# Attention steps of a decoder trunk: one broadcast VectorE product for the probabilities, and value products evacuated by ScalarE and added by GpSimd

## The chip, the cores and the metric

One Trainium2 chip, one core. The time is the device time of one launch in microseconds; the kernel before is given as the median of three runs. The engines are TensorE (PE in the profile, its weight loads PEld), VectorE (DVE), ScalarE (ACT), GpSimd (POOL) and the DMA queue of SyncE (SP). Each works through its own instruction list in order and waits on semaphores for the others.

## The reference

A two-layer causal decoder trunk over 512 tokens of 1024 features in float32. Layer 0 mixes tokens with a gated MLP in chunks of 128, then a gated MLP with a causal convolution of width 3, then a gated per-layer embedding. A shared key and value projection follows. Layer 1 has sliding-window attention over these, then the same two blocks again, then a final norm. The change lies in the attention:

```python
q = (xn @ w_q).reshape(B, nb, BLOCK, N_KV_HEADS, GQA_GROUP, HEAD_DIM)
scores = einsum('bnikgd,bnjkd->bnkgij', q, kblk) * HEAD_DIM ** -0.5
scores = scores - slopes * dist            # ALiBi
scores = where(valid, scores, -inf)        # 128 keys back, inside two blocks of 128
m = maximum(max(scores), sink)
e = exp(scores - m)
probs = e / (sum(e) + exp(sink - m))
out = einsum('bnkgij,bnjkd->bnikgd', probs, vblk)
return out.reshape(B, S, N_Q_HEADS * HEAD_DIM) @ w_o
```

There are 16 query heads of 64 features in 4 groups (4 heads share a key and value head), and 4 blocks of 128 tokens.

## The kernel before

The activations lie feature by token. Every large product is made of three matmuls on operands split in a rounded high part and the rest (`h*w` as `hi*hi + lo*hi + hi*lo`, L181 to L183), so each operand needs a cast on ScalarE (L154 for weights, L252 for activations) and a subtraction on VectorE (L155, L253).

The attention is a list of 16 steps, step i = 4g + n for head group g and token block n. The loop at L864 issues for each i: `scores(i)`, the work put beside step i (`fill`), `mix(i-2)`, `turn(i-1)` and `weights(i)`, so three steps are in flight. A scheduler then sets the order on each engine: it runs the program through with costs of its own, and `scores`, `turn` and `weights` have priority.

- `scores(i)`: eight matmuls (L781, L782) into two PSUM tiles `sc`; VectorE chooses between the two key blocks (`copy_predicated`, L784) and takes bias and row extreme (L788, four); ScalarE takes the exponential and its sum (L793, four). A small GpSimd copy (L774) puts the sink beside the row. The result lies in `prs`, in one of two buffers.
- `weights(i)`: the reciprocal of the sums `ds` (L801) and four products of 128x128, one per head: the first on VectorE (L807), three on ScalarE (L805).
- `turn(i)`: four TensorE transposes into a PSUM tile `tr` (L822), evacuated as high and low part (`pts`, L252 and L253). For n > 0, two GpSimd masks (L830) make a second pair for the previous block.
- `mix(i)`: two or four value matmuls (L844) into `pv`. Their left operand holds the values' high part in its first 64 columns and the low part in the last 64, so the upper and lower 64 partitions of `pv` have to be added. ScalarE copies the lower half to `side` (L848), VectorE adds the upper half to it, 64x256 twice (L852), placing the heads in the two partition halves. The sum is split: `oh` by ScalarE (L856), `ol` by GpSimd, for the last step by VectorE (L857). Both are columns of the tiles `o2`, two of them per head group.
- Beside the steps, TensorE has the query projections of the later groups (`project`, in step 0 to 9) and the merges, the w_o products on `o2` (`merge`, tile `o`, from step 10 and after the last step). A merge reads a whole `o2` tile, and so needs all four steps of its group.

PSUM has eight tiles, which all these share in turn.

Of the kernel before, what the change touches and what calls it, by code (L numbers as in the profile page):

```python
# [10 lines left out]
AF = mybir.ActivationFunctionType  # L11
ALU = mybir.AluOpType

P = 128
D = 1024
S = 512
# [10 lines left out]
GQ = HEADS // GROUPS  # L27
# [21 lines left out]
def tile_yoco(ctx: ExitStack, tc: tile.TileContext, t, out: bass.AP, out_b: bass.AP):  # L49
    nc = tc.nc  # L50
# [10 lines left out]
    def psum(name):  # L61
        return mmp.tile([P, S], F32, tag="mm", name=name)
# [166 lines left out]
    ps = psum("idle").rearrange("p (a b) -> p a b", a=4)  # L229
# [331 lines left out]
    for c in range(4):  # L561
# [4 lines left out]
        for j in range(2):  # L566
            m = 2 * c + j
            ps = ups[j]
# [24 lines left out]
    ps = psum("turned")  # L593
# [18 lines left out]
    sides = [slice(0, HD), slice(HD, P)]  # L612
# [184 lines left out]
    def weights(i):  # L797

        pr, sm = live[i]
        ds = at.tile([P, GQ], F32, tag="ds", bufs=2, name=f"ds{i}")  # L800
        nc.vector.reciprocal(ds, sm)  # L801
        for e in range(GQ):
            a, r = pr[:, e, :P], ds[:, e : e + 1]
            if e:
                nc.scalar.activation(a, a, AF.Copy, scale=r)  # L805
            else:
                nc.vector.tensor_scalar_mul(a, a, r)  # L807
        live[i] = pr

    def pair(name):  # L810
# [24 lines left out]
    def mix(i):  # L835
        g, n = steps[i]
        pts = live.pop(i)
        ps = psum(f"pv{i}")
        todo = []
        for b, halves in enumerate(pts):  # L840
            both_halves = (diffs[g][:, n - 1] if b else vt[:, n, g]).rearrange("p a d -> p (a d)")
            todo += [(both_halves, x) for x in halves]
        for j, (lhs, rhs) in enumerate(todo):
            nc.tensor.matmul(ps, lhs, rhs, start=j == 0, stop=j == len(todo) - 1)  # L844


        low = side[sides[0], i % 2 * S : (i % 2 + 1) * S]
        nc.scalar.copy(low, ps[sides[1], :])  # L848
        o = side[:, 2 * S + i % 2 * N : 2 * S + (i % 2 + 1) * N].rearrange("p (b t) -> p b t", b=2)
        a, low = (x.rearrange("p (b e t) -> p e b t", b=2, e=2) for x in (ps[sides[0], :], low))  # L850
        for e in range(2):
            nc.vector.tensor_add(o[sides[e]], a[:, e], low[:, e])  # L852
        cols = slice(n * P, (n + 1) * P)
        for b in range(2):
            oh, ol = o2[2 * g + b]
            nc.scalar.copy(oh[:, cols], o[:, b, :])  # L856
            (nc.vector if i == last - 1 else nc.gpsimd).tensor_sub(ol[:, cols], o[:, b, :], oh[:, cols].bitcast(F32))  # L857

    last = len(steps)
    side = at.tile([P, 4 * S], F32, tag="vtl", name="side")  # L860
# [3 lines left out]
    for i in range(last + 2):  # L864
        if i < last:
            with tc.high_priority():
                scores(i)
        if i <= last:
            fill(i)
        if i >= 2:  # L870
            mix(i - 2)
        if i > last:
            fill(i)
        if 0 <= i - 1 < last:
            with tc.high_priority():
                turn(i - 1)
        if i < last:
            with tc.high_priority():
                weights(i)
# [46 lines left out]
    for i in range(2):  # L926
# [4 lines left out]
        for q in range(2):  # L931
            ps = psum(f"ht{i}_{q}")
# [4 lines left out]
    for m in range(4):  # L937
        ps = psum(f"gate{4 + m}")[:, :N]
# [32 lines left out]
    def gate_t(i, n):  # L971

        c0, w = cuts[i][n]
        ps = psum(f"gt{i}_{n}")[:, :w]
        end = i == 1 and n == len(cuts[i]) - 1
        if end:
            nc.tensor.matmul(ps, rows[:, :P], rows[:, P : 3 * P], start=True, stop=False)
        mm3t(ps, xs, parts2 if c0 >= S else parts, c0 % S, w, 2 + i, first=not end)
        return ps
# [57 lines left out]
    ps = gate_t(0, 1)  # L1037
# [72 lines left out]
```

## Time and profile before

| | |
|---|---|
| median of three runs | 1141.24 us (1140.78 to 1141.5) |
| the profiled execution | 1141.22 us, span 1139.5 us |
| granted TensorE clock | 0.998 |
| TensorE busy | 1127.0 us, 99% of the span |
| VectorE, ScalarE, GpSimd busy | 749.6, 530.0, 107.7 us |
| attention steps | about 592 to 690 us of the span |

Times below are microseconds from the start of the span unless marked ns. A row of the timeline gives start, duration, engine, line, operation, output <- inputs, shapes and a count where like rows are merged; in brackets the idle time before it and what ended it. A busy TensorE is one with an instruction in flight: a matmul's record is longer than the distance to the next one's start. A row of groups gives busy time, mean duration in ns, and idle time before with what ended it. Where a group has "least/median/most", these are ns.

### The profile page before, as it was taken

Reading aid. Unit: us, or ns where it says so; the run is one execution under the profiler, and the core shown is the slowest. Engines: PE = TensorE matmul, PEld = TensorE weight load, DVE = VectorE, ACT = ScalarE, POOL = GpSimd, SP = SyncE. Lnnn points to the kernel's source line nnn. Section 1 sums busy time; section 2 is a strip of 40 time slices with the busy share of each in tenths; the row PEclk is TensorE's granted clock in tenths of the full one; section 3 lists DMA queues with packets and bytes.
Section 4 is the critical chain, followed back from the end, with each engine's and each line's share of the span. In section 5 each row is a group of like instructions: output and inputs, shape, how many; then the busy total and the mean of one; then the engine's idle time right before and its main releaser. Section 6 shows DMA issues by size and latency. Waiting matters only on the chain.

```text
span 1139.5 us, 13604 instructions
## 1 busy us (share of the span) xinstructions
PE 1127.0 (99%) x5266; PEld 940.5 (83%) x5266; DVE 749.6 (66%) x1158; ACT 530.0 (47%) x875; POOL 107.7 (9%) x175
## 2 busy tenths in 40 slices
PE   9999999999999999999999999999999999999997
PEld 7888888888888888888898878888888888888896
DVE  7366477763677367557988977777636763675675
ACT  6533344441344234445657985444313432355562
POOL 2000200000000000021213343000000000000222
PEclk9999999999999999999999999999999999999999
DMA  8422323223223322432224315223223233224302
GB/s 298 145 83 74 111 75 111 101 85 111 78 98 102 111 76 86 134 107 79 74 75 129 93 38 185 98 88 111 78 107 110 66 102 111 93 80 160 111 1 75
DMA packets 25776, 115.41 MB, mean 101 GB/s; under 512 B 2920, under 2 KB 8176, under 8 KB 16240
## 3 DMA queue, kind: packets, MB, share of 16 engines
q1 hardware_dynamic: 25152, 113.89, 29.8%
q8 instruction: 41, 0.67, 0.2%
q10 hardware_dynamic: 560, 0.66, 0.2%
q14 instruction: 23, 0.19, 0.1%
HBM read 108.24 MB, written 2.11 MB: 97 GB/s over the span
## 4 chain that ended last, share of the span: by engine, by line
PE 95%; DVE 2%; issue 1%; ACT 1%; DMA 1%; POOL 0%; SPq 0%; POOLq 0%; DVEq 0%; ACTq 0%
PE up L181 14%; PE up L183 14%; PE up L182 14%; PE d L183 8%; PE d L181 8%; PE d L182 8%; PE gate L181 2%; PE gate L183 2%; PE gate L182 2%; PE u L182 1%; PE u L183 1%; PE u L181 1%; PE o L182 1%; PE o L181 1%; PE o L183 1%; PE q L181 1%
## 5 line engine op out<-in xcount | busy, mean ns | idle before, releaser
L154 ACT CAST wh<-wraw 128x1024 fp32r<-128x1024 f32 (+2 forms) x197 | 202.0, 1028 | 264.6 <-PE d L182 131.0
L155 DVE TENSOR_TENSOR wl<-wraw,wh 128x1024 fp32r<-128x1024 f32 (+1 forms) x198 | 238.4, 1205 | 127.9 <-ACT wh L154 127.6
L181 PE MATMUL up<-nf00h,wh 128*128 128x512 f32 x352 | 137.1, 390 | 0.0
L181 PE MATMUL up<-nf10h,wh 128*128 128x512 f32 x352 | 137.0, 389 | 0.0
L182 PE MATMUL up<-nf00l,wh 128*128 128x512 f32 x352 | 136.9, 389 | 0.0
L183 PE MATMUL up<-nf00h,wl 128*128 128x512 f32 x352 | 136.9, 389 | 0.0
L183 PE MATMUL up<-nf10h,wl 128*128 128x512 f32 x352 | 136.9, 389 | 0.0
L182 PE MATMUL up<-nf10l,wh 128*128 128x512 f32 x352 | 136.9, 389 | 0.0
L181 PE MATMUL d<-ah,wh 128*128 128x512 f32 x352 | 136.9, 389 | 0.0
L182 PE MATMUL d<-al,wh 128*128 128x512 f32 x352 | 136.9, 389 | 0.0
L183 PE MATMUL d<-ah,wl 128*128 128x512 f32 x352 | 136.9, 389 | 0.0
L379 ACT ACTIVATE c<-hs,vec 128x512 f32<-128x512 f32 x88 | 71.5, 815 | 72.0 <-DVE hs L375 71.2
L380 DVE SCALAR_TENSOR_TENSOR c<-hs,vec,c 128x511 f32<-128x511 f32 x88 | 65.8, 749 | 34.5 <-ACT c L379 34.4
L355 DVE TENSOR_TENSOR h<-h,d 128x512 f32<-128x512 f32 x56 | 38.4, 686 | 73.8 <-PE d L183 73.8
L252 ACT CAST ah<-a 128x512 fp32r<-128x512 f32 x44 | 27.4, 622 | 109.5 <-DVE a L385 109.4
L183 PEld LDWEIGHTS up<-nf10h,wl 128*128 128x128 f32 x352 | 66.1, 188 | 13.8
L182 PEld LDWEIGHTS d<-al,wh 128*128 128x128 f32 x352 | 66.1, 188 | 13.8
L183 PEld LDWEIGHTS up<-nf00h,wl 128*128 128x128 f32 x352 | 66.1, 188 | 13.8
L183 PEld LDWEIGHTS d<-ah,wl 128*128 128x128 f32 x352 | 66.1, 188 | 13.7
L182 PEld LDWEIGHTS up<-nf00l,wh 128*128 128x128 f32 x352 | 66.1, 188 | 13.7
L182 PEld LDWEIGHTS up<-nf10l,wh 128*128 128x128 f32 x352 | 66.1, 188 | 13.7
L181 PEld LDWEIGHTS d<-ah,wh 128*128 128x128 f32 x352 | 66.1, 188 | 13.6
(454 smaller groups left out, 2061.7 us busy)
## 6 DMA issues: line engine op xcount, KB each, us to landing
wraw<-in_w_up SPq DMA_DIRECT2D x44, 1024.0 KB, 4.8
wraw<-in_w_down SPq DMA_DIRECT2D x16, 896.0 KB, 4.6
wraw<-in_w_down SPq DMA_DIRECT2D x8, 1024.0 KB, 4.8
wraw<-in_w_gate SPq DMA_DIRECT2D x8, 1024.0 KB, 4.8
wraw<-in_w_u SPq DMA_DIRECT2D x4, 1024.0 KB, 5.9
wraw<-in_w_out SPq DMA_DIRECT2D x4, 1024.0 KB, 4.8
wraw<-in_w_q SPq DMA_DIRECT2D x4, 1024.0 KB, 4.9
wraw<-in_w_o SPq DMA_DIRECT2D x4, 1024.0 KB, 4.9
```

What stands on the lines that cost most here:

```text
L154: nc.scalar.copy(hi, src)
L155: nc.vector.tensor_sub(low, src, hi.bitcast(F32))
L181: nc.tensor.matmul(ps, wh[:, a:b], xh, start=st, stop=False)
L182: nc.tensor.matmul(ps, wh[:, a:b], xl, start=False, stop=False)
L183: nc.tensor.matmul(ps, wl[:, a:b], xh, start=False, stop=en)
L252: nc.scalar.copy(hi, src)
L355: nc.vector.tensor_add(h[m], h[m], ps)
L379: nc.scalar.activation(c, hs, AF.Identity, bias=v("conv_b", l * 2 * NJ + col), scale=cw[2])
L380: nc.vector.scalar_tensor_tensor(c[:, 1:], hs[:, : S - 1], cw[1], c[:, 1:], op0=ALU.mult, op1=ALU.add)
```

## The change

Two places of the attention steps change, and nothing else.

In `weights` the four products become one: VectorE multiplies the whole 128 x 4 x 128 block of `prs` with `ds`, repeated along the last axis. ScalarE has no part in it any more.

In `mix` ScalarE copies both halves of `pv` to `side`, both into the same 64 partitions, the lower or the upper half in turn with the step. The two sums of 64x256, now with both inputs in SBUF, go to GpSimd. `oh` and `ol` stay where they were.

```diff
         nc.vector.reciprocal(ds, sm)
-        for e in range(GQ):
-            a, r = pr[:, e, :P], ds[:, e : e + 1]
-            if e:
-                nc.scalar.activation(a, a, AF.Copy, scale=r)
-            else:
-                nc.vector.tensor_scalar_mul(a, a, r)
+        a = pr[:, :, :P]
+        nc.vector.tensor_mul(a, a, ds.rearrange("p (e o) -> p e o", o=1).to_broadcast([P, GQ, P]))
...
-        low = side[sides[0], i % 2 * S : (i % 2 + 1) * S]
-        nc.scalar.copy(low, ps[sides[1], :])
         o = side[:, 2 * S + i % 2 * N : 2 * S + (i % 2 + 1) * N].rearrange("p (b t) -> p b t", b=2)
-        a, low = (x.rearrange("p (b e t) -> p e b t", b=2, e=2) for x in (ps[sides[0], :], low))
+        two = [side[sides[i % 2], x * S : (x + 1) * S] for x in range(2)]
+        for x in range(2):
+            nc.scalar.copy(two[x], ps[sides[x], :])
+        a, low = (x.rearrange("p (b e t) -> p e b t", b=2, e=2) for x in two)
         for e in range(2):
-            nc.vector.tensor_add(o[sides[e]], a[:, e], low[:, e])
+            nc.gpsimd.tensor_add(o[sides[e]], a[:, e], low[:, e])
```

In the changed kernel the product is L803, the copies L846, the sums L849, the transposes L818, the masks L826, the value matmuls L840, `oh` L853 and `ol` L854. The scheduler orders the instructions anew.

## The prediction

> **What bounds the kernel now.** I read the page's head first, then the busy time of each engine in stretches, then TensorE's waits, then the timeline of the stretch where they lie.
>
> ```profile
> PE 1127.0 (99%) x5266; PEld 940.5 (83%) x5266; DVE 749.6 (66%) x1158; ACT 530.0 (47%) x875; POOL 107.7 (9%) x175
> ```
>
> TensorE is the bound over the whole: 1127.0 us of a span of 1139.5. Whatever the change does to other engines counts only where TensorE waits for them. In stretches (columns: stretch, length, busy us of PE, PEld, DVE, ACT, POOL, granted clock, DMA):
>
> ```profile
> 640.00:650.00 10.00, 9.89 (x55) 8.17 (x54) 8.83 (x32) 9.30 (x29) 4.84 (x10) 1.00 0.24 52
> 650.00:660.00 10.00, 8.37 (x49) 6.62 (x50) 9.51 (x40) 9.79 (x37) 3.27 (x8) 1.00 0.25 54
> 660.00:670.00 10.00, 8.78 (x45) 6.76 (x44) 7.80 (x26) 8.85 (x31) 5.45 (x12) 1.00 0.30 106
> 670.00:680.00 10.00, 9.31 (x45) 7.33 (x46) 8.01 (x29) 7.92 (x30) 5.16 (x8) 1.00 0.01 2
> 600.00:690.00 90.00, 86.33 (x453) 70.80 (x452) 72.75 (x235) 72.77 (x236) 35.73 (x74) 1.00 0.35 104
> ```
>
> The attention steps (600 to 690 us) hold 90 - 86.33 = 3.67 us of idle TensorE, nearly all between 640 and 680, where ScalarE and VectorE are busy up to 98% and 95%. GpSimd is idle for more than half. The clock is full, so it plays no part. What TensorE waits for, from its list of waits and its timeline:
>
> ```profile
> PE tr L822 <- DVE prs L807: 1.7, 3, 0.8
> 639.83 0.39 PE L183 MATMUL q<-n11h,wl 128*128 128x512 f32 x1
> 640.06 0.39 PE L181 MATMUL q<-n11h,wh 128*128 128x512 f32 x1
> 649.50 0.39 PE L844 MATMUL pv<-pts,vt 128*128 128x512 f32 x1
> 650.68 0.41 PE L822 MATMUL tr<-ident,prs 128*128 128x128 f32 x2 [0.80 <-DVE prs L807]
> 662.11 0.50 PE L182 MATMUL o<-ol,wh 128*128 128x512 f32 x1 [0.71 <-POOL ol L857]
> 670.03 0.52 PE L822 MATMUL tr<-ident,prs 128*128 128x128 f32 x3 [0.53 <-DVE pts L253]
> 672.20 0.47 PE L844 MATMUL pv<-p13h,vt 128*128 128x512 f32 x1 [0.36 <-ACT prs L793]
> 672.92 0.50 PE L181 MATMUL o<-oh,wh 128*128 128x512 f32 x1 [0.26 <-ACT oh L856]
> ```
>
> Unstalled matmuls start 0.23 us apart (639.83, 640.06) though each record lasts 0.39, so each stall is 0.16 us longer than its idle mark: from 649.50 to 650.68 TensorE lost 1.18 - 0.23 = 0.95 us, not 0.80. There are three stalls of the transposes on the scaled probabilities (1.7 + 3 x 0.16 = 2.2 us), one where a merge (w_o product) waits for the last `ol` of step 7 (0.9), and three after step 11 (0.53 + 0.36 + 0.26 + 3 x 0.16 = 1.6). With the small ones the attention loses 3.67 + some 8 x 0.16 = 5.0 us. That is 0.44% of the time and all that this change can win.
>
> **The change part by part.** Groups from 590 to 692 us (last two figures before the idle time: busy us in all, mean ns of one), and the nearest rows for the new operations (ns: least, median, most):
>
> ```profile
> L793 ACT ACTIVATE prs<-prs,neg 128x129 f32<-128x129 f32 x64 | 25.2, 396 | 3.2 <-DVE neg L788 2.4 <-POOL ol L857 0.6
> L805 ACT ACTIVATE prs<-prs,ds 128x128 f32<-128x128 f32 x48 | 15.9, 395 | 0.0
> L807 DVE TENSOR_SCALAR prs<-prs,ds 128x128 f32<-128x128 f32 x16 | 6.5, 409 | 0.2
> L848 ACT COPY side<-pv 64x512 f32<-64x512 f32 x16 | 9.3, 583 | 2.9 <-PE pv L844 2.4
> L852 DVE TENSOR_TENSOR side<-pv,side 64x256 f32<-64x256 f32 x32 | 13.3, 416 | 3.8 <-ACT side L848 3.4
> L857 POOL TENSOR_TENSOR ol<-side,oh 128x128 fp32r<-128x128 f32 x30 | 14.1, 490 | 4.3 <-ACT oh L856 4.2
> L335 DVE TENSOR_TENSOR nf0dh<-ident,nf0rh x1: 684/684/684, 153.2 to 153.2; 128x512 fp32r<-128x512 f32 x1
> L912 POOL TENSOR_TENSOR facc<-facc,fsq x6: 737/741/1021, 1104.7 to 1113.4; 128x256 f32<-128x256 f32 x6
> 649.21 0.49 ACT L856 CAST oh<-side 128x128 fp32r<-128x128 f32 x2
> 649.58 0.87 POOL L857 TENSOR_TENSOR ol<-side,oh 128x128 fp32r<-128x128 f32 x2
> 652.12 0.40 PE L844 MATMUL pv<-pts,vt 128*128 128x512 f32 x1
> 653.90 0.58 ACT L848 COPY side<-pv 64x512 f32<-64x512 f32 x1
> 654.39 0.99 ACT L805 ACTIVATE prs<-prs,ds 128x128 f32<-128x128 f32 x3
> ```
>
> VectorE: 16 products of 128x128 (6.5 us) and 32 sums (13.3 us) go; 16 products of 128x512 with a broadcast factor come, priced by L335, which has that shape and that broadcast: 16 x 0.684 = 10.9. Net -8.9 us of 72.75.
>
> ScalarE: the three scalings of a step take 0.99 us end to end; the added copy takes 0.49, since the next instruction starts that long after it (653.90 to 654.39). Net -0.5 us a step, -8 us of 72.77 over 16 steps.
>
> GpSimd: 32 sums of 64x256 come. No row has 64 partitions, or an output in other partitions than the input; the nearest is L912, the same 256 elements on 128 partitions: 0.74 us, 32 x 0.74 = 23.7 us, so 35.73 becomes 59 of 90. Bounds: the 0.49 of a 128x128 `ol`, and L912's 1.02. I take 0.74, the row of equal length.
>
> So the two full engines are relieved by 0.5 us a step and the idle one is filled. Two chains per step change. *Scores to transposes*: reciprocal, then one VectorE product of 0.68 in place of 0.99 on ScalarE: the last transpose can go 0.3 us sooner, the first 0.3 later. *Value product to merge*: copy 0.58, sums 0.83, `oh` 0.49, `ol` 0.87 becomes copies 1.07, sums 1.48, `oh` 0.49, `ol` 0.87: 2.8 us becomes 3.9. A late sum also holds what stands behind `oh` in ScalarE's queue, the next exponentials and evacuations: between copies and `oh` stand mostly two exponentials (0.8), so ScalarE waits some 0.7 us for the sums where it is not late by other work. That can eat its whole 0.5 us a step. VectorE loses such a wait: the sums stood in its queue ahead of scores.
>
> TensorE's instruction order is the same up to the transposes of step 9; then merges move ahead. Merge matmuls between the transposes of steps 9, 10, 11, 12, 13, 14, 15: before 6, 3, 21, 0, 3, 33; after 12, 9, 9, 0, 18, 18.
>
> *Up to the transposes of step 11*: six more merges at steps 10 and 11 are 1.4 us each, against stalls of 0.5 to 0.95; at step 9 ScalarE's new order has all four exponentials ahead of step 8's evacuation, where the last stood behind. So the three stalls on the products go: -2.2 us. The merge on step 7's `ol` now comes six merges (1.4), one value matmul (0.2) and a block of transposes and scores (650.68 to 652.12, 1.4) after that step's value product, 3.0 us, against 3.5 to the first half of `ol`: 0.5 in place of 0.9. Together -2.6.
>
> *After step 11*: the first merge that needs its `oh` comes 8 scores, 4 transposes and two value matmuls after that step's last value product.
>
> ```profile
> 668.63 0.63 PE L844 MATMUL pv<-pts,diff 128*128 128x512 f32 x2
> 672.58 0.50 ACT L856 CAST oh<-side 128x128 fp32r<-128x128 f32 x2
> 676.40 1.19 DVE L155 TENSOR_TENSOR wl<-wraw,wh 128x1024 fp32r<-128x1024 f32 x1
> 676.55 1.78 POOL L857 TENSOR_TENSOR ol<-side,oh 128x128 fp32r<-128x128 f32 x2 [0.28 <-ACT oh L856]
> ```
>
> Before, `oh` began 672.58 - 669.26 = 3.3 us after those matmuls. Now ScalarE has ahead of it the evacuation of step 12, two copies, three exponentials and the evacuation of step 13, which itself waits for that step's product; and TensorE has no merges to put between. Counted through the queues with the durations above: the first value matmul of step 12 waits 1.5 us (its evacuation stands behind step 13's exponentials, and these behind step 10's `oh`), step 13's transposes 0.8 for the product, the merge 1.25 for `oh` and 0.7 for `ol`, which stands behind masks on GpSimd. That is 4.2, where 1.6 and 0.5 of small ones stood: +2.1, good to 2 us.
>
> *End of the steps*: step 15's chain.
>
> ```profile
> 684.37 1.38 POOL L830 TENSOR_SCALAR_AFFINE_SELECT pts<-pts 128x512 fp32r<-128x512 f32 x2 [2.72 <-ACT pts L252]
> 685.55 0.75 PE L844 MATMUL pv<-pts,diff 128*128 128x512 f32 x2
> 687.01 0.87 DVE L852 TENSOR_TENSOR side<-pv,side 64x256 f32<-64x256 f32 x2 [1.24 <-ACT side L848]
> 687.91 0.50 ACT L856 CAST oh<-side 128x128 fp32r<-128x128 f32 x2 [0.93 <-DVE side L852]
> 689.57 0.39 PE L181 MATMUL o<-oh,wh 128*128 128x512 f32 x1
> ```
>
> Before, `oh` began 1.66 us ahead of the merge at 689.57 that reads it, so nothing waited. Now GpSimd has in order: the masks to 685.75, step 14's sums to 687.23, its `ol` after `oh` to 688.45, step 15's sums to 689.93; then half of `oh` and VectorE's `ol`, 690.5. TensorE stalls about 0.9.
>
> Sum: -2.6 + 2.1 + 0.9 = +0.4 us, and some 0.6 for the port below: +1.0 on the profiled run's 1141.22 (span 1139.5, 1.7 around it; the median is 1141.24, the same): **1142.2 us**.
>
> **The port between VectorE and GpSimd.** Rows:
>
> ```profile
> 649.95 0.58 DVE L807 TENSOR_SCALAR prs<-prs,ds 128x128 f32<-128x128 f32 x1
> L807 DVE TENSOR_SCALAR prs<-prs,ds x16: 269/396/598, 595.5 to 677.5; 128x128 f32<-128x128 f32 x16
> L249 DVE SCALAR_TENSOR_TENSOR nf10l<-h,vec,nf10h x8: 740/750/1790, 693.1 to 714.9; 128x512 fp32r<-128x512 f32 x8
> ```
>
> L807 takes 0.27 us alone and 0.58 when two GpSimd sums run: it ended at 650.53, just after they did at 650.45. L249 goes from 0.74 to 1.79. The other way, an `ol` pair took 1.78 us, not 0.88, behind L155 (676.40). [...]
>
> **Rivals.** *The port decides (slower).* The new product, on the path to the transposes, waits out a pair of sums (up to 1.48 us), or these wait for it (0.9). It decides if that falls on steps 9 to 15, where no queries cover it: seven times 0.9 = 6.3 us, less the 2.6 won: +3.7 and, with 0.9 at the end, 1145.8 us. For it: GpSimd goes from 40% to 66% busy. Against: the product mostly falls where the sums wait for their copies.
>
> *The relief comes through (faster).* If the sums' wait is hidden behind exponentials, the stalls up to step 11 go whole (-3.1), after step 11 it stays as it was, and the end costs up to 0.5: about 1138.6 us. For it: the two engines that are full lose 0.5 us a step. Against: `oh` waits in ScalarE's queue.
>
> *Nothing moves.* The merges moved ahead cover as much as the longer chain costs: 1141.2.
>
> **How the numbers follow.** A measurement of this kernel can tell about 0.2%, 2.3 us, from no change. Forecast 0.48, port 0.30, relief 0.15, nothing 0.07. The forecast's own uncertainty (the counted 4.2 us, the 0.49 to 1.02 of a sum) is some 2.5 us, so of its 0.48 I put 0.09 beyond slower and 0.03 beyond faster. Faster 0.03 + 0.11 = 0.14; slower 0.09 + 0.25 = 0.34; the rest 0.52. Range 1138.0 to 1146.5: from the relief case, half a microsecond below, to just above the port case.
>
> **What would show it.** Right: no wait of the transposes of steps 9 to 11 on the product; TensorE waits of 2 us or more in all for `oh` and `ol` of step 11, and near 1 us for step 15's; the product's median near 0.7 with a maximum over 1.2; the sums near 0.74. Wrong: stalls before step 9, where TensorE now has none; sums at 1 us or above; or idle TensorE under 2 us from 600 to 690.

## The result, and the profile after

1154.86 us median of four runs (1154.01 to 1155.13), against 1141.21 for the kernel before beside it: ratio 1.0119, 95% interval 1.0101 to 1.0136. The change costs 13.7 us; 1142.2 was forecast, and the range ended at 1146.5. The profiled run took 1154.01 us, its span is 1152.3.

The stretches that were shown of before, now of the changed kernel (same columns):

```profile
640.00:650.00 10.00, 10.00 (x45) 8.22 (x44) 6.59 (x23) 7.37 (x25) 5.91 (x11) 0.83 0.25 55
650.00:660.00 10.00, 7.21 (x37) 5.90 (x35) 7.92 (x28) 8.10 (x24) 6.11 (x11) 0.86 0.12 26
660.00:670.00 10.00, 8.27 (x41) 6.23 (x39) 6.35 (x23) 6.99 (x25) 7.86 (x13) 0.96 0.42 133
670.00:680.00 10.00, 6.97 (x41) 5.61 (x41) 6.33 (x20) 7.65 (x24) 7.40 (x12) 1.00 0.00 1
600.00:690.00 90.00, 79.74 (x404) 65.27 (x403) 64.58 (x200) 63.19 (x192) 54.89 (x93) 0.94 0.29 83
```

TensorE is idle for 10.26 us of the 90 (3.67 before). VectorE and ScalarE are less busy than before (64.58 and 63.19, from 72.75 and 72.77), GpSimd more: the work moved as intended, and yet neither VectorE nor ScalarE is full, a sign of engines waiting for each other in turn. And the granted clock, 1.00 throughout before, is 0.83 to 0.96 in three of the stretches. What TensorE waits for:

```profile
PE pv L840 <- ACT pts L252: 6.5, 4, 2.3
PE o L181 <- ACT oh L853: 2.4, 2, 1.6
PE tr L818 <- DVE prs L803: 0.5, 1, 0.5
```

The waits of the transposes (`tr`) on the scaled probabilities went from 1.7 us to 0.5. A wait that did not exist takes their place: the value matmuls wait for ScalarE's evacuation of the transposes, 6.5 us. Why ScalarE is late there is seen in the groups of the steps (here from 590 to 705 us):

```profile
L849 POOL TENSOR_TENSOR side<-side 64x256 f32<-64x256 f32 x32 | 26.4, 826 | 13.1 <-ACT side L846 11.8
L846 ACT COPY side<-pv 64x512 f32<-64x512 f32 x32 | 18.6, 581 | 2.7 <-PE pv L840 2.1
L803 DVE TENSOR_TENSOR prs<-prs,ds 128x512 f32<-128x512 f32 x16 | 11.8, 736 | 0.4
L853 ACT CAST oh<-side 128x128 fp32r<-128x128 f32 x32 | 8.1, 296 | 17.2 <-POOL side L849 17.2
L801 DVE RECIPROCAL ds<-sm 128x4 f32<-128x4 f32 x16 | 2.8, 176 | 17.4 <-ACT prs L793 17.4
```

and the same two last groups of before:

```profile
L856 ACT CAST oh<-side 128x128 fp32r<-128x128 f32 x32 | 8.0, 294 | 3.0 <-DVE side L852 2.8
L801 DVE RECIPROCAL ds<-sm 128x4 f32<-128x4 f32 x16 | 2.8, 173 | 2.0 <-ACT prs L793 1.7
```

ScalarE stands 17.2 us in front of `oh`, waiting for GpSimd's sums (3.0 before, for VectorE's), in 15 waits of 1.15 us on average. VectorE's reciprocal waits 17.4 us for the exponentials (2.0 before). One step in the timeline, engine by engine in order of start:

```profile
651.32 0.59 ACT L846 COPY side<-pv 64x512 f32<-64x512 f32 x1
652.03 0.63 POOL L826 TENSOR_SCALAR_AFFINE_SELECT u7l<-pts 128x512 fp32r<-128x512 f32 x1
652.45 0.39 ACT L793 ACTIVATE prs<-prs,neg 128x129 f32<-128x129 f32 x1
652.64 1.53 POOL L849 TENSOR_TENSOR side<-side 64x256 f32<-64x256 f32 x2
654.21 0.50 ACT L853 CAST oh<-side 128x128 fp32r<-128x128 f32 x2 [1.27 <-POOL side L849]
654.61 0.40 ACT L793 ACTIVATE prs<-prs,neg 128x129 f32<-128x129 f32 x1
655.01 0.39 ACT L793 ACTIVATE prs<-prs,neg 128x129 f32<-128x129 f32 x1
655.39 1.03 ACT L154 CAST wh<-wraw 128x1024 fp32r<-128x1024 f32 x1
655.52 0.18 DVE L801 RECIPROCAL ds<-sm 128x4 f32<-128x4 f32 x1 [1.63 <-ACT prs L793]
655.73 0.69 DVE L803 TENSOR_TENSOR prs<-prs,ds 128x512 f32<-128x512 f32 x1
656.45 0.58 ACT L252 CAST pts<-tr 128x512 fp32r<-128x512 f32 x1
657.09 0.64 PE L840 MATMUL pv<-pts,vt 128*128 128x512 f32 x1 [2.25 <-ACT pts L252]
```

The copies end at 651.91. GpSimd has a mask first, then the two sums, until 654.17. `oh` stands in ScalarE's queue between the step's second and third exponential, so the last two exponentials wait with it, and the reciprocal and the product after them. The evacuation of the step before needs none of these: its last transpose started at 651.78. But it stands behind them in ScalarE's queue, and behind a weight cast of 1.03 us as well. TensorE loses 2.4 us from 654.45.

Masks are not the only thing that makes the sums late. Two pairs of sums took 2.66 and 2.65 us where most took some 1.5, at 633.64 and here:

```profile
658.61 0.68 DVE L658 TENSOR_TENSOR qf<-qf,qhi 128x512 fp32r<-128x512 f32 x1
658.90 2.65 POOL L849 TENSOR_TENSOR side<-side 64x256 f32<-64x256 f32 x2 [3.16 <-ACT side L846]
659.75 1.22 DVE L155 TENSOR_TENSOR wl<-wraw,wh 128x1024 fp32r<-128x1024 f32 x1
661.58 0.50 ACT L853 CAST oh<-side 128x128 fp32r<-128x128 f32 x2 [1.92 <-POOL side L849]
661.93 0.50 PE L181 MATMUL o<-oh,wh 128*128 128x512 f32 x1 [1.65 <-ACT oh L853]
```

Each time VectorE ran two subtractions with two inputs beside them, of the queries (L658) and of the weights (L155), which the kernel before has too. `oh` then waits 1.9 us in place of some 0.7, and right behind the two pairs come TensorE's losses of 1.7 us (from 636.33) and 2.3 (from 659.87).

The clock falls behind such stalls:

```profile
654.00:656.00 2.00, 0.83 (x4) 0.36 (x2) 0.44 (x2) 1.79 (x7) 1.23 (x4) 1.00 0.00 0
656.00:658.00 2.00, 0.91 (x4) 0.75 (x4) 1.63 (x4) 1.95 (x4) 0.00 (x0) 0.82 0.00 0
658.00:660.00 2.00, 2.00 (x11) 1.99 (x10) 2.00 (x11) 1.61 (x6) 1.04 (x2) 0.50 0.59 131
```

By the trace's clock records TensorE ran at half clock from 640.23, 657.30 and 681.19, each time for 3.41 us. Matmuls of 512 columns start 0.43 us apart there (from 641.26), and 0.23 apart behind it (from 643.75). So a stretch costs 1.71 us of full speed, the three 5.1, as far as TensorE did not stand still anyway.

### The profile page after: what moved, and what is told of

Read it like the earlier page. It is cut to its first block, busy times and chain, and to the rows that moved or that the text cites. A ratio compares the mean times of both kernels' runs of the same rounds, so it can differ in the third digit from the quotient of the medians.

```text
span 1152.3 us, 13565 instructions
## 1 busy us (share of the span) xinstructions
PE 1132.5 (98%) x5266; PEld 943.6 (82%) x5266; DVE 743.7 (65%) x1126; ACT 526.3 (46%) x843; POOL 136.3 (12%) x207
## 5 line engine op out<-in xcount | busy, mean ns | idle before, releaser
L155 DVE TENSOR_TENSOR wl<-wraw,wh 128x1024 fp32r<-128x1024 f32 (+1 forms) x198 | 239.0, 1208 | 129.8 <-ACT wh L154 129.5
L183 PEld LDWEIGHTS d<-ah,wl 128*128 128x128 f32 x352 | 66.1, 188 | 13.7
L182 PEld LDWEIGHTS up<-nf00l,wh 128*128 128x128 f32 x352 | 66.1, 188 | 13.7
L181 PEld LDWEIGHTS up<-nf10h,wh 128*128 128x128 f32 x352 | 66.1, 188 | 13.7
L181 PEld LDWEIGHTS d<-ah,wh 128*128 128x128 f32 x352 | 66.1, 188 | 13.7
```

Source lines behind the costliest of these rows:

```text
L155: nc.vector.tensor_sub(low, src, hi.bitcast(F32))
L181: nc.tensor.matmul(ps, wh[:, a:b], xh, start=st, stop=False)
L182: nc.tensor.matmul(ps, wh[:, a:b], xl, start=False, stop=False)
L183: nc.tensor.matmul(ps, wl[:, a:b], xh, start=False, stop=en)
```

## The experiments

Theory 1 is the chain above. Rival 1 is what the prediction calls the port: VectorE and GpSimd holding each other up, taken from rows like the pair of `ol` that took 1.78 us behind L155 in the kernel before, not 0.88. The traces show such durations, not their cause. Rival 2 is the second ScalarE copy or the new instruction order, rival 3 the VectorE product itself. Each kernel is timed against the kernel before on the same chip; the medians of before were 1141.19 to 1141.40.

**The two halves of the change, each alone.** `product_only` has the new `weights` and the old `mix`:

> The first half of the change alone: one VectorE product a step in place of three ScalarE scalings and one VectorE scaling; the value products' halves are joined as before (one ScalarE copy, VectorE sums). Theory 1 (ScalarE is held at `oh` by GpSimd's late sums, and with it the exponentials, the product and the evacuation): this half is harmless, 1138 to 1142.5 us, ScalarE's wait at `oh` stays at 3 us in 32, and no TensorE wait for the value products' evacuation above 1 us in all. Rival 3 (the longer VectorE product itself delays the transposes): 1147 us or more, with TensorE waiting for the product.

`sums_only` has the old `weights` and the new `mix`:

> The second half alone: two ScalarE copies and GpSimd sums, while the probabilities are scaled as before (three ScalarE scalings, one VectorE scaling), so VectorE has no product with two SBUF inputs in the steps. Theory 1: the loss is here; 1152 to 1160 us, ScalarE waits over 12 us in all at `oh` for the sums (17.2 in the changed kernel), and is 0.5 us a step fuller still. Rival 1 (the port: the VectorE product and the sums lock each other out): without that product the loss goes, 1141 to 1146 us, and the sums' mean falls from 0.83 to 0.75 us.

Measured: `product_only` 1146.53 us (ratio 1.0039, 1.0024 to 1.0053), `sums_only` 1154.17 (1.0115, 1.0100 to 1.0130). In `sums_only` the sums and the two waits are:

```profile
L853 POOL TENSOR_TENSOR side<-side 64x256 f32<-64x256 f32 x32 | 23.7, 740 | 8.7 <-ACT side L850 7.2
L857 ACT CAST oh<-side 128x128 fp32r<-128x128 f32 x32 | 8.3, 294 | 10.0 <-POOL side L853 10.0
L801 DVE RECIPROCAL ds<-sm 128x4 f32<-128x4 f32 x16 | 2.8, 176 | 14.4 <-ACT prs L793 14.3
```

In this kernel the sums take the forecast 0.74 us, only one of them as much as 1.07, and yet the loss is all but the same. So rival 1 is not needed for a loss of this size. It is not refuted as a part of it: of the six sums over 0.9 us in the changed kernel only two ran beside the new product, and the longest stand beside L658 and L155, as shown. The way to the loss differs, too: here 3.1 us of TensorE's waits are for masks that stand in GpSimd's queue:

```profile
PE pv L844 <- POOL pts L830: 3.1, 2, 2.0
```

The wait at `oh`, 10.0, is under the 12 expected: ScalarE has its scalings back and is later by itself. `product_only` fits neither theory: ScalarE waits 6.2 us at `oh`, but has that time: the reciprocal waits only 1.7 us, TensorE is idle for only 1.9 us more than before from 590 to 700, and still 5.3 us are lost. Its stretches from 666 to 682 us:

```profile
666.00:670.00 4.00, 2.77 (x15) 1.82 (x14) 3.40 (x10) 3.39 (x9) 1.06 (x3) 1.00 0.01 2
670.00:674.00 4.00, 2.36 (x13) 1.93 (x13) 3.48 (x15) 2.76 (x10) 1.27 (x2) 0.78 0.00 0
674.00:678.00 4.00, 3.41 (x9) 1.89 (x8) 3.61 (x14) 2.80 (x13) 1.42 (x2) 0.50 0.00 0
678.00:682.00 4.00, 4.00 (x13) 3.32 (x12) 1.74 (x4) 1.48 (x5) 2.53 (x6) 0.50 0.01 2
```

TensorE's idle time crowds from 667 to 673, and then the clock is at half for 10.24 us, three times 3.41. In this kernel's order no merge stands between the transposes of steps 12 and 13, and only two matmuls of one ahead of step 14's.

**The sums back on VectorE.** From the changed kernel:

```
-            nc.gpsimd.tensor_add(o[sides[e]], a[:, e], low[:, e])
+            nc.vector.tensor_add(o[sides[e]], a[:, e], low[:, e])
```

> The changed kernel with one edit: the two sums of a step are VectorE's again, from the two ScalarE copies. Theory 1: the sums come within about 1 us of the copies, the wait at `oh` falls from 17.2 to under 6 us, 1140 to 1146 us. Rival 2 (the second ScalarE copy, or the instruction order that came with the change): the copy is still there and the order up to the transposes of step 9 is nearly the same, so 1150 us or more.

1143.43 us (1.0019, 1.0010 to 1.0029), clock 1.00, a wait at `oh` of 2.7 us and at the reciprocal of 2.8. With both ScalarE copies and the VectorE product in place, 11.4 of the 13.7 us are gone. So most of the loss is not the second copy but the sums on GpSimd, with the order of instructions that they bring. What is left, 2.2 us, shows as transposes that wait 2.9 us for the product (1.7 for the products before) and one evacuation that costs 1.3.

**One sum each**, the first on VectorE, the second on GpSimd:

> The changed kernel with one edit: of a step's two sums the first is VectorE's and the second GpSimd's, so that they run side by side. A dose of the same thing: two sums on GpSimd gave a wait of ScalarE at `oh` of 17.2 us and 1154.9 us, none gave 2.7 us and 1143.4 us. Theory 1 (the time goes with the wait): a wait of 6 to 11 us and 1145 to 1151 us, part of it again in stretches of 3.4 us at clock 0.50 if stalls of 2 us or more within 3 us come back. Rival 1 (the port: any sum on GpSimd beside VectorE's two-input instructions costs): the wait stays at 12 us or more and the time at 1151 us or more.

```profile
L853 ACT CAST oh<-side 128x128 fp32r<-128x128 f32 x32 | 7.9, 296 | 7.8 <-POOL side L849 7.0 <-DVE side L849 0.7
L801 DVE RECIPROCAL ds<-sm 128x4 f32<-128x4 f32 x16 | 2.8, 174 | 5.9 <-ACT prs L793 5.8
```

1145.82 us (1.0035, 1.0022 to 1.0047): the time goes with the wait, 2.7, 7.8 and 17.2 us of it giving 2.2, 4.4 and 13.7 us over the kernel before. The wait has no fixed price, though: `sums_only` lost 13.0 us with 10.0 of it.

**`oh` behind all four exponentials** (the same work; its place in ScalarE's queue changes, and with it the scheduler's order on the other engines in a few places):

```
+    def halves(i):    # oh and ol of step i
...
+        if 3 <= i < last:
+            with tc.issue_after(exp):    # the step's last exponential
+                halves(i - 3)
```

> The changed kernel with one edit: each step's two `oh` casts are queued on ScalarE behind all four exponentials of the step beside them instead of between the second and the third; nothing is added or taken away, and the sums stay on GpSimd beside the VectorE product. Theory 1: GpSimd's sums then run behind 0.8 us more of exponentials, the wait at `oh` falls from 17.2 to 4 to 9 us, VectorE's reciprocal no longer waits 17 us for the exponentials, and the time comes to 1141 to 1147 us. Rival 1 (port) and rival 2 (copy): same sums, same product, same copies, so 1151 us or more.

1150.21 us (1.0079, 1.0064 to 1.0094). The wait at `oh` falls to 8.8 and the reciprocal's to 5.5, as expected, but only 4.7 us are won where some 8 or more were expected. TensorE's waits for the evacuations are halved, from 6.9 us to 3.2, not gone. And a second cost has grown: the merges wait 4.5 us for `oh` and `ol` in place of 2.4, and the clock is at half for 6.83 us from 657.36, toward the end of the longest of these waits.

**`oh` on GpSimd**, so that ScalarE waits for no sum:

```
-            nc.scalar.copy(oh[:, cols], o[:, b, :])
+            nc.gpsimd.tensor_copy(oh[:, cols], o[:, b, :])
```

> The changed kernel with one edit: `oh` is cast by GpSimd, right behind its sums, so that ScalarE waits for no sum at all. TensorE's and VectorE's instruction order is the changed kernel's to the last instruction. Theory 1 (ScalarE held at `oh`): VectorE's reciprocal waits under 6 us for the exponentials in place of 17.4, TensorE's waits for the value products' evacuation fall from 6.9 to under 2 us, and the time falls by at least 4 us to 1142 to 1150; what stays is the longer way to the merges, which now also holds two casts on GpSimd. Rival 1 (the port): GpSimd is fuller still, so 1155 us or more. Rival 2 (the second copy, the order of TensorE): both are kept, so 1152 to 1157 us.

1148.75 us (1.0062, 1.0044 to 1.0080). TensorE's waits:

```profile
PE o L181 <- POOL oh L853: 5.0, 3, 3.0
PE pv L840 <- ACT pts L252: 0.7, 2, 0.4
```

VectorE's order is the changed kernel's, and so is TensorE's but for one place: twelve merge matmuls now stand ahead of a value matmul of step 12 (at 683.70 in the changed kernel). The 6.9 us of waits for ScalarE's evacuation (`pts` and `p4h`) fall to 0.7, and all of them came before that place. Theory 1 holds for them. What is left is the second cost: the merges wait 5.0 us for `oh`, 3.0 of it for step 7's, and the clock is at half for 6.83 us from 655.73. Step 7's sums took 2.64 us here, again beside L658 and L155, so some 1.1 of the 3.0 us look like rival 1's.

**Merges against the crowded idle time.** `product_fill` is `product_only` with four products of merge 3 moved ahead, `before_fill` the kernel before with the same (the three numbers of a merge are its output block and the range of `o2` tiles):

```
-        13: [(merge, 2, 1, 4)],
+        13: [(merge, 2, 1, 4), (merge, 3, 0, 4)],
...
-        16: [(merge, 3, 0, 6)],
+        16: [(merge, 3, 4, 6)],
```

> The first half of the change alone, with one more edit: the first four of six products of merge 3 are given to loop step 13 instead of 16, so that TensorE has 12 more matmuls (2.7 us) between steps 11 and 13, where the first half alone left it without other work and where its stalls crowd (3.7 us lost from 667 to 673), after which the granted clock was 0.50 from 672.25 to 682.75. No work is added or taken away. If the clock falls because idle time crowds: it stays at 1.00, and the time comes to 1139 to 1142.5 us, below the 1146.5 of the first half alone by at least 3 us. If the clock has another cause: the same 1144 to 1147 us with some stretch at 0.50.

> The kernel before with the same move of merge 3's first four products and nothing else; the control for the run beside it. The clock was 1.00 there already, so the move can win at most the 1.5 us of stalls between steps 11 and 13: 1139.5 to 1142 us, clock 1.00.

1142.04 us (1.0005, 0.9995 to 1.0015) and 1141.74 (1.0005, 0.9996 to 1.0015). In `product_fill`, where the stalls crowded:

```profile
666.00:670.00 4.00, 4.00 (x26) 3.47 (x25) 3.41 (x9) 3.71 (x9) 1.75 (x3) 1.00 0.01 2
670.00:674.00 4.00, 2.05 (x11) 1.10 (x9) 3.97 (x14) 2.33 (x8) 0.00 (x0) 1.00 0.48 156
674.00:678.00 4.00, 3.29 (x17) 2.39 (x17) 3.74 (x15) 2.30 (x11) 2.55 (x4) 1.00 0.25 107
```

The clock stays at 1.00 (the mean of a run is 0.996 to 0.999, against 0.993 to 0.998 for `product_only`), and 4.5 us come back without any work taken away, while the same move wins nothing for the kernel before. So the loss of `product_only` was idle time brought together, most of it through the clock.

**The merges dealt out anew**, so that those on `o2[0]` and `o2[1]`, ready long ago, come first:

```
+        10: [(merge, 0, 0, 2), (merge, 1, 0, 2), (more,)],
+        11: [(merge, 2, 0, 2), (merge, 0, 2, 4), (more,)],
+        12: [(merge, 1, 2, 4)],
+        13: [(merge, 2, 2, 4), (merge, 3, 0, 4)],
...
+        16: [(merge, 3, 4, 6)],
```

> The changed kernel with `oh` cast by GpSimd (as in the run before) and with the merges dealt out anew over the loop steps: the products of merges 0 to 2 with `o2[0]` and `o2[1]` (ready long ago) come first, those that need step 7's `oh` and `ol` one or two steps later, and merge 3's first four go to loop step 13. Same work. The 5.0 us in which the merges waited for `oh` (3.0 of them for step 7's) were the rest of the loss, with the two stretches of 3.4 us at clock 0.50 behind them. Theory 1 with this second term: both kinds of wait are gone or cut by half, the clock is at 1.00 and the time 1140.5 to 1144 us. If something else in the sums on GpSimd costs time (the port; GpSimd at 79 us of 110): 1146 us or more.

> The changed kernel with the same dealing-out of merges alone; `oh` stays on ScalarE between the exponentials. Theory 1: the first stalls, on the evacuations of steps 4 to 6 (3.0 us, before any merge can run), stay, and so does one stretch at clock 0.50 behind them; the later ones shrink, since TensorE has more merges beside them: 1146 to 1151 us, slower than the run beside it. If only the merges' order were to blame: the same 1140.5 to 1144 us as that run.

Both miss the times of theory 1. `oh_gpsimd_fill` takes 1147.44 us (1.0055, 1.0038 to 1.0072), in the range given for something else in the sums on GpSimd. The clock is at 1.00 in its profiled run (1146.42), so what that run loses is not the clock: TensorE still waits 3.3 us for `oh`, and now 2.3 for masks, which stand behind the sums and casts on GpSimd:

```profile
PE o L181 <- POOL oh L853: 3.3, 3, 1.3
PE pv L840 <- POOL pts L826: 2.3, 2, 1.3
```

`after_fill` takes 1157.13 (1.0140, 1.0125 to 1.0155), slower than the changed kernel. More merges beside the steps leave the chain itself as long as it was, and at one place two waits at `oh` now follow each other before the same step's last exponentials:

```profile
677.50 0.50 ACT L853 CAST oh<-side 128x128 fp32r<-128x128 f32 x2 [1.70 <-POOL side L849]
680.88 0.50 ACT L853 CAST oh<-side 128x128 fp32r<-128x128 f32 x2 [1.50 <-POOL side L849]
682.20 0.18 DVE L801 RECIPROCAL ds<-sm 128x4 f32<-128x4 f32 x1 [4.37 <-ACT prs L793]
685.34 1.22 PE L840 MATMUL pv<-pts,vt 128*128 128x512 f32 x2 [4.37 <-DVE pts L253]
```

One stall of 4.5 us stands there, and the clock is at half for 6.83 us from 683.54. So this other order of the merges alone does not mend the changed kernel. In `oh_gpsimd_fill` GpSimd's queue itself is on TensorE's path, and one pair of sums took 2.67 us beside L658 and L155; how much of its loss is rival 1's is not separated.

**The product alone with the merges dealt out anew**, and the kernel before with the same as control:

> The first half of the change alone (the single VectorE product) with the same dealing-out of merges: TensorE has 12 matmuls of merges at each of loop steps 10 and 11 where it had 6. The stalls of the transposes there (0.82 and 1.32 us) and the wait for step 7's `ol` should shrink or go, clock 1.00: 1138 to 1141 us, which would beat both kernels. If the product itself were too slow for the path to the transposes: 1142 us or more, with stalls on it.

> The kernel before with the same dealing-out of merges, the control for the run beside it: three stalls of the transposes on the scaled probabilities (0.95, 0.73, 0.67 us) and one on step 7's `ol` (0.98) lie where the merges are added: 1138 to 1141 us, clock 1.00. The difference to the run beside it is then what the single product is worth by itself: between -1 and +1 us.

`product_fill2` takes 1140.02 us (0.9989, 0.9979 to 0.9998), `before_fill2` 1140.78 (0.9996, 0.9986 to 1.0005). In neither do the transposes wait for a product any more; in the first, TensorE's longest waits are 1.2 us for `ol` and 0.8 for an evacuation. It is 1.2 us below the kernel before, by an interval that just excludes no change; the difference to its control is 0.8, which these intervals do not separate.

## Why the prediction was wrong, step by step

The stalls below are those over 0.3 us beyond the unstalled spacing of the matmuls, from their starts.

*Prices of the operations.* Right. The product's median is 0.692 us, its maximum 1.07 (0.684 forecast, the maximum over 1.2 was not reached); the sums' median is 0.732 (0.74); by the groups, VectorE's product (11.8 us) replaces 19.8 us, and ScalarE's added copy (9.3) replaces 15.9: -8.0 and -6.6 us (-8.9 and -8 forecast).

*"So the three stalls on the products go: -2.2", together -2.6 up to the transposes of step 11.* The three went; one of 0.7 us came at step 11. The sum is wrong: from 3.3 us the stalls there went to 8.4, of which 5.4 on the evacuations of steps 4, 5, 7 and 8 and 2.3 on `oh` of step 7 (0.5 forecast). That is +5.0 in place of -2.6, the largest error. The step that failed is the sentence on ScalarE's queue: it "waits some 0.7 us for the sums", which "can eat its whole 0.5 us a step". Two things were wrong in it. The size: 1.15 us on average. In six steps the wait was 0.6 to 0.9, as forecast. In four it was 1.05 to 1.42, because the sums stood behind masks in GpSimd's queue (0.73 us in the step shown), where the working began them at the end of the copies; in two it was 1.9, because the sums themselves took 2.65 us. The other three waits lie in the last steps. And the sign of the net, which weighs more: the wait was set against ScalarE's saved work and dropped from the sum. But saved work counts only where ScalarE is full, while the wait lies ahead of two exponentials on the path to the product, and ahead of the evacuation for which the value matmuls wait. The prediction named stalls before step 9 as the mark of its being wrong; they begin at step 4.

*After step 11, "+2.1, good to 2 us".* Right in size, in part by luck: stalls of 3.9 us (4.2 forecast), where 2.0 stood, are +1.8. The places differ: the value matmul of step 12 lost 2.3 us (1.5 forecast), the transposes around it 1.5 (0.8), waiting for VectorE's half of the evacuation and not for the product, and no wait for `oh` of step 11 came.

*"End of the steps: about 0.9".* Right, by the queue that was counted: masks, step 14's sums, its `ol`, step 15's sums; the merge on step 15's `oh` lost 0.91 us.

*The port, 0.6.* The working gives no count for this figure, and no run shows it. The rival expected the new product to collide with the sums, and that was small: two sums beside a product (1.11 and 1.07 us, median 0.73), and two products, one of them beside sums (1.07 and 1.02, median 0.69), were longer by 0.3 to 0.4 us each. What it did not name weighs more: the two pairs beside L658 and L155, each longer by 1.1 us, ahead of 4.0 of the 8.4 us above. No run takes these two collisions away by themselves, so how much of the 4.0 us is theirs stays open. The rival gave the right side mostly by luck.

*Not in the prediction: the clock.* "The clock is full, so it plays no part" was read from before and carried over to a kernel with other stalls. The rest of the excess, spacings wider by less than 0.3 us each, is +5.0 us, 4.1 of it inside the three stretches of half clock, which could cost 5.1. With +5.0, +1.8 and +0.9 it makes 12.7 of the 12.8 us by which the profiled span grew.

How much of the clock's part would come back with ScalarE's wait alone is not separated; no run here has the wait and a full clock.

## What to carry to other kernels

When work moves to an idle engine, look at who waits for the result in an in-order queue and what stands behind the waiter: `oh` cost nothing by itself, but the exponentials and the evacuation behind it set the pace of the step. Price such a wait from the other engine's queue, with what is ahead of the work there and what VectorE runs at the same time (the pairs of sums beside L658 and L155 took 2.66 and 2.65 us, most some 1.5), and do not set it against work saved on the waiting engine. And count stalls not only by their sum: in `product_only` TensorE was idle for 1.9 us more than before and 5.3 us were lost, with the clock at half for 10.24 us behind idle time that crowded from 667 to 673; with merges dealt in between, 4.5 of them came back.

## What the runs showed of the hardware

Across these fourteen traces every stretch of half clock in the steps is 3.41 us long or a whole multiple (6.83, 10.24), and in the changed kernel the stretches start whole multiples of it apart (640.23, 657.30 and 681.19 are 5 and 7 apart). In the 3.41 us ahead of each of its three falls TensorE was not idle throughout: it started matmuls of 2,560, 2,048 and 640 columns in all, by the starts and shapes of the timeline, against a median of 7,680 over the whole run in such lengths. The first of the three (from 636.82) holds most of the stall of 1.7 us from 636.33, and then transposes and short matmuls. Laid on the same spacing, no length of this trace with 4,096 columns or more at full clock was followed by a fall (4,096 were started from 660.71). But in `exp_first` some 2,560 were started from 674.43 to 677.84, and the clock stayed at 1.00. So the three falls came behind little work, and no number of columns parts them from the rest in these traces; no run varied the columns by themselves.

From one kernel to another the stretches need not start whole multiples apart: 640.23 in the changed kernel and 672.27 in `product_only` are 9.4 lengths apart. And the clock of one kernel differs from run to run, with its time. The six runs of `half` took 1144.50 and 1144.56 us at a mean clock of 0.999, and 1145.62 to 1146.43 at 0.997; the runs of `product_only` took 1143.96 at 0.998, 1145.14 at 0.995, and 1146.53 to 1146.70 at 0.993 to 0.994. Which stretches of half clock the other runs had, their means do not show.
